# Attention scores of a diffusion layer: the low part of the queries multiplies only the high part of the keys, two key blocks in the two row halves of the array

## The chip, the cores and the metric

The kernel runs on one core of a Trainium2 chip. The metric is the device time of one execution, in microseconds (us); of several runs the median is given. A profile is one further execution with the hardware profiler on. Its own time stands beside its span, the time from its first to its last recorded instruction.

## The reference: what is computed

One layer of a diffusion backbone over 1024 latent tokens of width 1024, with 256 context tokens in front. Each layer normalizes and modulates the tokens, projects them with one combined matrix, feeds the columns to two groups of heads (chunkwise retention, and differential attention), projects their outputs back, and ends with a gated MLP with a short convolution. The change lies in the differential attention, cut here to what matters:

```python
def diff_attention(q, k, v, lam):
    """q (B,H,2,Lq,d), k (B,H,2,Lk,d), v (B,H,Lk,dv); softmax(q1k1)-lam*softmax(q2k2)."""
    scale = d ** -0.5
    def attend(qb):
        s = jnp.einsum('bhmqd,bhmkd->bhmqk', qb, k).astype(jnp.float32) * scale
        p = jax.nn.softmax(s, axis=-1)
        a = p[:, :, 0] - lam * p[:, :, 1]
        return jnp.einsum('bhqk,bhke->bhqe', a.astype(v.dtype), v)
...
    k_all = jnp.concatenate([dk_c, dk_l], axis=3)
    v_all = jnp.concatenate([dv_c, dv_l], axis=2)
```

There are H = 4 heads, two score maps m = 0, 1 per head, a head width d = 64, 1024 queries (latent tokens) and 1280 keys (256 context, 1024 latent). Softmax and the sum over keys do not depend on the order of the keys, as long as the keys and the values have the same order.

## The kernel before, in words

**Stages.** The kernel runs in this order: modulation vectors and normalized inputs; the input projection, weight block by weight block, with the retention worked beside it; the differential attention (from some 496 us to 695 us of the profile); the output projection; the two MLP products. Weight and token operands are split into a high part, rounded to the fast matmul type, and a low part, the rest; `passes` (L126 to L131) multiplies high by high, high by low and low by high.

**Queries and keys of the attention.** They are made by `transposed` (L433) and `rotated` (L407), which ends in `split_store` (L400). That one copies the high part into slot 0 of a tile `xhl` on ScalarE, the low part into slot 1 on VectorE, and writes both to DRAM through SyncE's queue. `dq_d[h]` and `dk_d[h]` in DRAM have the shape 64 x 2 (map m) x 2 (slot) x tokens. Of the keys, the context's come first (L625, columns 0 to 255) and the latents' behind them (L627, from column 256). The values `dv_d` have the same order (L568 and L605). Both halves `hf` of 512 latent tokens are handled alike.

**How they lie on the chip.** `load` (L796), through GpSimd's queue, fills the key tile `ks` as 128 partitions x 2 maps x 1280 keys: partitions 0 to 63 hold slot 0 (the high part of the 64 dimensions) and partitions 64 to 127 hold slot 1 (the low part). The query tile `qhl` holds the same queries in both partition halves: index i = 0 is the high part, i = 1 the low part. So one matmul over 128 partitions gives query part i times high plus low keys.

**One unit of the attention** is one head and one block of 128 queries, 32 units in all (`class Unit`, L714). `scores` (L722 to L727) fills, for one map m, the PSUM tile `pA` (1280 of 1536 columns, three banks) in three column blocks of 512, 512 and 256, each with two matmuls (i = 0 starts the sum, i = 1 ends it): six weight loads and six matmuls over the full array. Then follow `least` (the minimum over the keys, VectorE, L730), `exp` (ScalarE, L734), `ratio` and `combine` (the two maps into one, VectorE, L742), `turn` and `turned` (10 transposes on TensorE, L747, copied out by ScalarE, L753), `values` (the product with the values in full float32, 20 matmul instructions, L759), and the normalization of the output.

**What sets the order.** The units are pipelined: `TAU` (L64) gives every step a due time in units, and the loop at L865 issues, turn by turn, the steps of several units sorted by the fraction of their due time. `in_order` (L117) then fixes this order on TensorE, VectorE, ScalarE and SyncE. On TensorE one turn is: scores of map 1, four transposes, the 20 matmuls with the values, two transposes, scores of map 0, four transposes, the transpose of an output (`pty`, L782). There is one `pA` tile per map, so the scores of a map wait until `exp` of the unit before has read the tile. The early steps of the first two units (`EARLY`, L62) are issued at L821, between the last blocks of the query projection.

**A product elsewhere that splits the array.** The modulation vectors (`mod_part`, L488 to L499) are made with weights of 32 columns only. Four such matmuls write four groups of 32 PSUM partitions, so each uses a quarter of the array's columns. They stand between ordinary matmuls of the first projection.

Of the kernel before, what the change touches and what calls it, by code (L numbers as in the profile page):

```python
# [12 lines left out]
ALU = mybir.AluOpType  # L13
# [7 lines left out]
L = 1024  # L21
NT = L // P
LC = 256
NTC = LC // P
LK = LC + L
# [42 lines left out]
def r32(ap):  # L68
    return ap.bitcast(F32)
# [3 lines left out]
def kernel(  # L73
# [16 lines left out]
    nc = tc.nc  # L90
    mm = nc.tensor.matmul
# [34 lines left out]
    def passes(ps, lt, rt, first, last, more=False):  # L126
        lh, ll = lt
        rh, rl = rt
        mm(ps, lh, rh, start=first, stop=False, skip_group_check=more)  # L129
        mm(ps, lh, rl, start=False, stop=False, skip_group_check=more)  # L130
        mm(ps, ll, rh, start=False, stop=last, skip_group_check=more)  # L131
# [6 lines left out]
    dk_d = [dr.tile([64, 2, 2, LK], F32, name=f"dk{h}") for h in range(H)]  # L138
# [13 lines left out]
    with ExitStack() as p1:  # L152
        pctx = p1.enter_context(ExitStack())
        first = ExitStack()
# [10 lines left out]
        def mm_tile(name):  # L165
            return next(banks["mm"]).tile([P, 512], F32, name=name, tag="mm")
# [23 lines left out]
        def stream_parts(b):  # L190
            sl = []

            def more():
                kk = len(sl)
                sl.append(split_slice(w_in[b][:, 2 * kk : 2 * kk + 2, :]))

            def get(k, c0, c1):
                return tuple(t[:, k % 2, c0:c1] for t in sl[k // 2])

            return get, more  # L200

        def stream_block(b):
            get, more = stream_parts(b)
            for _ in range(KD // 2):
                more()
            return get
# [10 lines left out]
        def load_rope(kind):  # L217
            rtab = rp.tile([P, 2, L], F32, name="rtab")
            nc.sync.dma_start(out=rtab, in_=rope[:, kind])
            return rtab  # L220
# [147 lines left out]
        def tick():  # L368
            side["due"] += side["rate"]
            while side["due"] >= 1.0:  # L370
                side["due"] -= 1.0
                next(side["g"], None)

        def beside(g, rate, due=0.0):
            for _ in side["g"]:
                pass
            side.update(g=g, rate=rate, due=due)

        def natural(wget, lhs, tiles, finish):
            for t in tiles:  # L380
                pt = mm_tile("pn")
                for k in range(KD):
                    passes(pt, lhs(t, k), wget(k, 0, 512), k == 0, k == KD - 1)
                    tick()
                finish(t, pt)

        def store_to(dst, func=AF.Copy, scale=1.0, c0=0, center=False):
            def fin(t, pt):
                st = ev.tile([P, 4, P], F32, name="st", bufs=3)
                nc.scalar.activation(st.rearrange("p h e -> p (h e)"), pt, func, scale=scale)  # L390
                if center:
                    mu = ev.tile([P, 32], F32, name="mu")[:, 0:4]
                    nc.vector.tensor_reduce(out=mu, in_=st, axis=AX.X, op=ALU.add)
                    nc.vector.tensor_scalar(out=mu, in0=mu, scalar1=1.0 / P, scalar2=None, op0=ALU.mult)
                    nc.vector.tensor_tensor(out=st, in0=st, in1=mu.unsqueeze(2).to_broadcast([P, 4, P]), op=ALU.subtract)
                nc.sync.dma_start(out=dst(c0 + t), in_=st.rearrange("p h e -> p (h e)"))

            return fin

        def split_store(src, dst):  # L400
            n = src.shape[-1]
            hl = ev.tile([P, 2, 512], F32R, name="xhl")
            nc.scalar.copy(hl[:, 0, :n], src)
            nc.vector.tensor_tensor(out=hl[:, 1, :n], in0=src, in1=r32(hl[:, 0, :n]), op=ALU.subtract)
            nc.sync.dma_start(out=dst.rearrange("p m a l -> (p m) a l"), in_=r32(hl[:, :, :n]))

        def rotated(pt, dst, rtab, blk, scale, col0, h, hf):  # L407
            xa = ev.tile([P, 512], F32, name="xa")
            xb = ev.tile([P, 512], F32, name="xb")
            for q in (0, 64):  # L410
                nc.scalar.activation(xb[q : q + 64, :], pt[64 - q : P - q, :], AF.Copy, scale=scale)
            cs = rtab[:, 0, hf * 512 : (hf + 1) * 512]
            sn = rtab[:, 1, hf * 512 : (hf + 1) * 512]
            nc.vector.scalar_tensor_tensor(out=xa, in0=pt, scalar=scale, in1=cs, op0=ALU.mult, op1=ALU.mult)
            nc.vector.tensor_tensor(out=xb, in0=xb, in1=sn, op=ALU.mult)
            nc.vector.tensor_tensor(out=xa, in0=xa, in1=xb, op=ALU.add)
            c0 = col0 + hf * 512
            if blk == 32:
                split_store(xa, dst[h][:, :, :, c0 : c0 + 512])
            else:  # L420
                nc.sync.dma_start(out=dst[h][:, c0 : c0 + 512], in_=xa)
            return xa

        def natural_copy(xa, h, hf):
            pk = pst.tile([P, 4, P], F32, name="pk", tag="tr")
            for i in range(4):
                nc.tensor.transpose(pk[:, i, :], xa[:, i * P : (i + 1) * P], ident)
            st = ev.tile([P, 4, P], F32, name="st", bufs=3)
            nc.scalar.copy(st, pk)
            for i in range(2):  # L430
                nc.sync.dma_start(out=kvg_d[1 + 2 * hf + i][:, 0, :, h * P : (h + 1) * P], in_=st[:, 2 * i : 2 * i + 2, :])

        def transposed(wget, dst, rtab, blk, scale, col0, order, nat=False):  # L433
            todo = None
            for h, hf in order:
                pt = mm_tile("pl")
                for k in range(KD):
                    passes(pt, wget(k, h * P, (h + 1) * P), tuple(hT[a][hf][:, k, :] for a in range(2)), k == 0, k == KD - 1)
                    tick()
                    if todo and k == KD - 2:  # L440
                        natural_copy(*todo)
                xa = rotated(pt, dst, rtab, blk, scale, col0, h, hf)
                todo = (xa, h, hf) if nat else None
            if todo:
                natural_copy(*todo)
# [27 lines left out]
        by_head = [(h, hf) for h in range(H) for hf in range(2)]  # L473
        m2c = p1.enter_context(ExitStack())

        with ExitStack() as p0:
# [57 lines left out]
            wget, more = stream_parts(6)  # L534
# [30 lines left out]
                    modulate(xs, d, 0, hT[0][1][:, d, :], hT[1][1][:, d, :])  # L565
                    yield

            store = store_to(dv_row, c0=NTC)  # L568
            for i in range(2):
                for q in range(2):  # L570
                    t = 2 * i + q
# [30 lines left out]
                for t in ts:  # L602
                    store(t, part[t])
            side["rate"] = 0.6
            natural(wget, ctx_lhs, range(NTC), store_to(dv_row))  # L605
            beside(iter(()), 0.0)
        rc = late.enter_context(tc.tile_pool(name="rc", bufs=1))
        gn = rc.tile([P, 2, 512], F32, name="gn")
# [9 lines left out]
        rtab = load_rope(1)  # L618
        natural(wget, lat_lhs, range(4, NT), store)
        wg = stream_block(5)  # L620
        for h in range(H):
            pt = mm_tile("pc")
            for k in range(KD):
                passes(pt[:, :LC], wg(k, h * P, (h + 1) * P), tuple(cT[a][:, k, :] for a in range(2)), k == 0, k == KD - 1)
            split_store(pt[:, :LC], dk_d[h][:, :, :, 0:LC])  # L625
        modulation2(0)
        transposed(wg, dk_d, rtab, 32, 1.0, LC, by_head)  # L627
        with tc.tile_pool(name="rc0", bufs=1) as r0:
            lp = r0.tile([P, 4, 64], F32, name="lp")
            nc.sync.dma_start(out=lp.rearrange("p a b -> p (a b)"), in_=rows[0, R_LAM : R_LAM + 256].partition_broadcast(P))  # L630
# [44 lines left out]
        wg = stream_block(2)  # L675
# [3 lines left out]
        wg = stream_block(1)  # L679
# [5 lines left out]
        rtab = load_rope(0)  # L685
# [3 lines left out]
        wg = stream_block(3)  # L689
# [7 lines left out]
        wg = stream_block(0)  # L697
        beside(outputs(), 1.19, -14.5)
        transposed(wg, [q[:, 0] for q in rqk_d], rtab, 64, 1.0, 0, by_head)
        rtab = load_rope(1)  # L700
        wg = stream_block(4)
# [12 lines left out]
        class Unit:  # L714
# [7 lines left out]
            def scores(self, m):  # L722
                self.pa[m] = pss[m].tile([P, 1536], F32, name="pA")
                qs = slice(self.qt % 4 * P, (self.qt % 4 + 1) * P)
                for c0, c1 in ((0, 512), (512, 1024), (1024, LK)):
                    for i in range(2):
                        mm(self.pa[m][:, c0:c1], self.q[:, m, i, qs], self.k[:, m, c0:c1], start=(i == 0), stop=(i == 1))  # L727

            def least(self, m):
                nc.vector.tensor_reduce(out=self.mt[:, m : m + 1], in_=self.pa[m][:, :LK], axis=AX.X, op=ALU.min)  # L730
# [128 lines left out]
    with ExitStack() as p2:  # L859
# [3 lines left out]
        start = len(nc.cur_bb.bb.instructions)  # L863
        order = sorted(TAU.items(), key=lambda it: it[1] % 1.0)
        for n in range(n_units + 8):  # L865
# [6 lines left out]
            if n in (8, 10, 12, 14):  # L872
                a, i = divmod(n // 2 - 4, 2)
# [98 lines left out]
    with ExitStack() as p3:  # L972
        ps = p3.enter_context(tc.tile_pool(name="ps3", bufs=2, space=PSUM))
        for n in range(2):
# [3 lines left out]
            for t in range(NT):  # L978
                pt = ps.tile([P, 512], F32, name="po3", tag="mm")
# [3 lines left out]
                dst = x1[t][:, n * 512 : (n + 1) * 512]  # L983
# [75 lines left out]
    chain, second, first, fifth, third = {}, {}, {}, {}, {}  # L1059
# [25 lines left out]
    with ExitStack() as p4:  # L1085
# [79 lines left out]
        last = None  # L1165
        for j in range(NF):
# [8 lines left out]
            last = blk  # L1175
# [5 lines left out]
        def flat(t):  # L1181
            return t.rearrange("p a b -> p (a b)")
# [9 lines left out]
        c1 = [bank(f"c1_{t}", psB if t < 2 else psC) for t in range(4)]  # L1192
        c2 = [bank(f"c2_{t}", psA) for t in range(4)]
        for m in range(2):
            pa = flat(raw_load("wra", a_d[0][m].rearrange("p c (a b) -> p (c a) b", b=P)))
# [228 lines left out]
```

## Time and profile before

| | |
|---|---|
| median of 3 runs | 1433.39 us (1433.27 to 1436.08) |
| profiled execution | 1438.13 us, span 1436.3 us |
| mean granted TensorE clock | 0.989 |
| TensorE matmul busy | 1380.4 us, 96% of the span |
| TensorE weight loads busy | 1144.8 us, 80% |
| VectorE busy | 994.2 us, 69% |
| ScalarE busy | 728.8 us, 51% |
| GpSimd busy | 288.2 us, 20% |

How to read a profile: PE is TensorE's matmuls, PEld its weight loads, DVE VectorE, ACT ScalarE, POOL GpSimd, SP SyncE. L727 is line 727 of the kernel, and `out<-in` names the tiles that an instruction writes and reads. A timeline row gives the start, the time from the first start to the last end, the engine, the line and the count of merged instructions. The recorded time of a matmul is longer than the distance to the next one, since matmuls are pipelined; costs on TensorE are therefore read from start to start. The chain is the sequence of work that ended last, followed back from the end.

### The profile page before, as it was taken

The page shows a single profiled execution, that of the slowest core. Times are in us where ns is not written, and L with a number is a line of the kernel's source. Part 1 is how long each engine was busy: PE and PEld are TensorE (multiplying, and loading weights), DVE is VectorE, ACT ScalarE, POOL GpSimd, SP SyncE. Part 2 cuts the span into 40 slices and gives each one's busy share as a digit, 9 for nine tenths or more (in the row PEclk, how much of TensorE's full clock was granted, in tenths as well). Part 3 has the DMA queues.
Part 4 walks back from the last instruction along what each step waited for, and adds up shares of the span by engine and source line. Part 5 has one row for each costly group of instructions (what it writes and reads, how often), then busy time and mean ns, then how long its engine had stood idle before and what let it go on. Part 6 is the DMA issues. An engine that isn't in the chain of part 4 may idle for free.

```text
span 1436.3 us, 19187 instructions
## 1 busy us (share of the span) xinstructions
PE 1380.4 (96%) x6924; PEld 1144.8 (80%) x6924; DVE 994.2 (69%) x1432; ACT 728.8 (51%) x1386; POOL 288.2 (20%) x321
## 2 busy tenths in 40 slices
PE   6899999999989899999999999999999999999996
PEld 2687887788878789999888778888888888888885
DVE  3566755343666599888346997888778777998457
ACT  3534412343465488998314754555555545455533
POOL 1220000000645323431201143222222330000001
PEclk9999999999999999999999999999999999999998
DMA  8557755365465767570512222223222235953224
GB/s 313 220 178 243 250 180 190 115 194 176 136 208 192 202 149 174 132 146 1 220 52 88 74 95 108 98 110 110 102 86 88 108 110 174 397 204 102 98 96 175
DMA packets 109798, 218.79 MB, mean 152 GB/s; under 512 B 9156, under 2 KB 49604, under 8 KB 108808
## 3 DMA queue, kind: packets, MB, share of 16 engines
q1 hardware_dynamic: 101544, 192.67, 38.7%
q0 software_dynamic: 8160, 24.91, 7.7%
q8 instruction: 54, 0.88, 0.3%
q14 instruction: 40, 0.33, 0.1%
HBM read 160.13 MB, written 57.41 MB: 151 GB/s over the span
## 4 chain that ended last, share of the span: by engine, by line
PE 78%; DVE 7%; issue 5%; DMA 5%; ACT 2%; POOL 2%; SPq 0%; POOLq 0%; DVEq 0%; ACTq 0%
PE chain L129 5%; PE chain L130 5%; PE chain L131 5%; PE pv L759 5%; PE pA L727 4%; PE c L130 4%; PE c L131 4%; PE c L129 4%; PE pn L130 3%; PE pn L129 3%; PE pn L131 3%; PE pl L131 3%; PE pl L130 3%; PE pl L129 3%; PE third L130 2%
## 5 line engine op out<-in xcount | busy, mean ns | idle before, releaser
L129 PE MATMUL chain<-T,whi 128*128 128x512 f32 x264 | 103.7, 394 | 4.7 <-ACT ua L1140 3.9
L129 PE MATMUL pl<-hT,whi 128*128 128x512 f32 x256 | 108.2, 422 | 0.0
L130 PE MATMUL chain<-T,whi 128*128 128x512 f32 x264 | 103.5, 392 | 0.0
L131 PE MATMUL chain<-T,wlo 128*128 128x512 f32 x264 | 103.1, 391 | 0.0
L131 PE MATMUL pl<-hT,wlo 128*128 128x512 f32 x256 | 101.8, 398 | 0.0
L130 PE MATMUL pl<-hT,whi 128*128 128x512 f32 x256 | 101.7, 397 | 0.0
L730 DVE TENSOR_REDUCE mt<-pA 128x1 f32<-128x1280 f32 x64 | 95.1, 1489 | 3.0 <-PE pA L727 1.2
L727 PE MATMUL pA<-ks,qhl 128*128 128x512 f32 (+1 forms) x384 | 89.6, 369 | 2.2 <-ACT p L734 2.2
L131 PE MATMUL c<-whi,ghl 128*128 128x512 f32 x232 | 90.4, 390 | 0.0
L130 PE MATMUL c<-wlo,ghl 128*128 128x512 f32 x232 | 90.3, 389 | 0.0
L129 PE MATMUL c<-whi,ghl 128*128 128x512 f32 x232 | 90.3, 389 | 0.0
L734 ACT ACTIVATE p<-pA,mt 128x1280 f32<-128x1280 f32 x64 | 85.5, 1336 | 8.4 <-DVE mt L730 8.3
L898 ACT CAST whi<-cmb 128x512 fp32r<-128x512 f32 x62 | 38.6, 622 | 86.5 <-PE chain L130 66.9
L129 PE MATMUL pn<-whi,hT 128*128 128x512 f32 x192 | 79.2, 412 | 0.0
L727 PEld LDWEIGHTS pA<-ks,qhl 128*128 128x128 f32 x384 | 67.6, 189 | 14.4 <-ACT p L734 3.0
L1053 POOL TENSOR_TENSOR cmb<-wrb 128x512 f32<-128x512 f32 x20 | 27.8, 1392 | 247.7 <-DMA wrb<-w_up 155.6
L759 PE MATMUL pv<-va,aT 128*128 128x128 f32 x640 | 77.1, 276 | 0.1
L130 PE MATMUL pn<-wlo,hT 128*128 128x512 f32 x192 | 76.2, 397 | 0.0
L131 PE MATMUL pn<-whi,hT 128*128 128x512 f32 x192 | 75.3, 395 | 0.5 <-DVE hT L531 0.5
L899 DVE TENSOR_TENSOR wlo<-cmb,whi 128x512 fp32r<-128x512 f32 x62 | 59.5, 963 | 23.2 <-ACT whi L898 23.2
L759 PEld LDWEIGHTS pv<-va,aT 128*128 128x128 f32 x640 | 74.0, 192 | 1.0 <-DVE yT L788 0.6
L115 POOL TENSOR_TENSOR sm<-sm,mhalf 128x1 f32<-128x1 f32 x26 | 16.1, 619 | 278.3 <-DVE sm L114 278.1
(302 smaller groups left out, 3820.5 us busy)
## 6 DMA issues: line engine op xcount, KB each, us to landing
wm<-w_mod SPq DMA_DIRECT2D x32, 512.0 KB, 4.4
raw<-w_in SPq DMA_DIRECT2D x28, 512.0 KB, 4.3
wra<-w_up SPq DMA_DIRECT2D x24, 512.0 KB, 3.3
wrb<-w_up SPq DMA_DIRECT2D x23, 512.0 KB, 3.6
W<-w_down SPq DMA_DIRECT2D x44, 256.0 KB, 5.9
ad<-s SPq DMA_DIRECT2D x20, 512.0 KB, 3.5
wra<-ad SPq DMA_DIRECT2D x20, 512.0 KB, 3.4
kvs<-kvg SPq DMA_DIRECT2D x36, 256.0 KB, 3.3
```

What stands on the lines that cost most here:

```text
L115: nc.gpsimd.tensor_tensor(out=out_ap, in0=out_ap, in1=mhalf[:, :n], op=ALU.pow)
L129: mm(ps, lh, rh, start=first, stop=False, skip_group_check=more)
L130: mm(ps, lh, rl, start=False, stop=False, skip_group_check=more)
L131: mm(ps, ll, rh, start=False, stop=last, skip_group_check=more)
L727: mm(self.pa[m][:, c0:c1], self.q[:, m, i, qs], self.k[:, m, c0:c1], start=(i == 0), stop=(i == 1))
L730: nc.vector.tensor_reduce(out=self.mt[:, m : m + 1], in_=self.pa[m][:, :LK], axis=AX.X, op=ALU.min)
L734: nc.scalar.activation(self.p[m], self.pa[m][:, :LK], AF.Exp, scale=-1.0, bias=self.mt[:, m : m + 1], accum_out=self.s[:, m : m + 1])
L759: mm(self.pv, self.aT[:, c, :], self.v[:, c, :], start=(c == 0), stop=(c == NKT - 1))
L898: nc.scalar.copy(hi, src)
L899: nc.vector.tensor_tensor(out=lo, in0=src, in1=r32(hi), op=ALU.subtract)
L1053: nc.gpsimd.tensor_tensor(out=s1, in0=b1, in1=b2, op=ALU.add)
```

## The change

The low part of the queries no longer multiplies the low part of the keys in the first two key blocks. For these 1024 keys the i = 0 matmul stays as it was, over all 128 partitions. The i = 1 matmuls become two matmuls over 64 partitions each: key block 0 takes partitions 0 to 63 of query and key, key block 1 takes partitions 64 to 127. So that the high part of the keys lies in the right half, the latent keys move to the front (columns 0 to 1023, the context behind them), and the second half of the latents stores its low part in slot 0 and its high part in slot 1. The last block of 256 keys, now the context, keeps both full matmuls, and they are issued ahead of the two half ones. The values in DRAM follow the new order of the keys.

```diff
-        def split_store(src, dst):
+        def split_store(src, dst, first=0):
             n = src.shape[-1]
             hl = ev.tile([P, 2, 512], F32R, name="xhl")
-            nc.scalar.copy(hl[:, 0, :n], src)
-            nc.vector.tensor_tensor(out=hl[:, 1, :n], in0=src, in1=r32(hl[:, 0, :n]), op=ALU.subtract)
+            nc.scalar.copy(hl[:, first, :n], src)
+            nc.vector.tensor_tensor(out=hl[:, 1 - first, :n], in0=src, in1=r32(hl[:, first, :n]), op=ALU.subtract)
             nc.sync.dma_start(out=dst.rearrange("p m a l -> (p m) a l"), in_=r32(hl[:, :, :n]))
...
-                split_store(xa, dst[h][:, :, :, c0 : c0 + 512])
+                split_store(xa, dst[h][:, :, :, c0 : c0 + 512], hf if dst is dk_d else 0)
...
-            store = store_to(dv_row, c0=NTC)
+            store = store_to(dv_row)
...
-            natural(wget, ctx_lhs, range(NTC), store_to(dv_row))
+            natural(wget, ctx_lhs, range(NTC), store_to(dv_row, c0=NT))
...
-            split_store(pt[:, :LC], dk_d[h][:, :, :, 0:LC])
+            split_store(pt[:, :LC], dk_d[h][:, :, :, L:LK])
         modulation2(0)
-        transposed(wg, dk_d, rtab, 32, 1.0, LC, by_head)
+        transposed(wg, dk_d, rtab, 32, 1.0, 0, by_head)
...
             def scores(self, m):
                 self.pa[m] = pss[m].tile([P, 1536], F32, name="pA")
                 qs = slice(self.qt % 4 * P, (self.qt % 4 + 1) * P)
-                for c0, c1 in ((0, 512), (512, 1024), (1024, LK)):
-                    for i in range(2):
-                        mm(self.pa[m][:, c0:c1], self.q[:, m, i, qs], self.k[:, m, c0:c1], start=(i == 0), stop=(i == 1))
+                pa = self.pa[m]
+                for c0, c1, last in ((0, 512, False), (512, 1024, False), (1024, LK, True)):
+                    for i in range(1 + last):
+                        mm(pa[:, c0:c1], self.q[:, m, i, qs], self.k[:, m, c0:c1], start=(i == 0), stop=(i == 1))
+                for g in range(2):
+                    half = slice(64 * g, 64 * g + 64)
+                    mm(pa[:, 512 * g : 512 * g + 512], self.q[half, m, 1, qs], self.k[half, m, 512 * g : 512 * g + 512], start=False, stop=True)
```

## The prediction

> **What bounds the kernel now.** The page's first part says that TensorE is busy for 96% of the span, but that is a mean. I therefore went to the table by stages for the attention, where the only edited instructions that cost time lie. Its columns after the stretch are its length, then the busy time (and count) of PE, PEld, DVE, ACT and POOL, the granted clock, the DMA share and GB/s.
>
> ```profile
> PE 1380.4 (96%) x6924; PEld 1144.8 (80%) x6924; DVE 994.2 (69%) x1432; ACT 728.8 (51%) x1386; POOL 288.2 (20%) x321
> ...
> 550.00:590.00 40.00, 40.00 (x299) 37.37 (x298) 35.78 (x50) 36.08 (x87) 12.44 (x25) 1.00 0.64 160
> 590.00:630.00 40.00, 39.89 (x294) 36.37 (x292) 34.54 (x49) 38.01 (x89) 18.59 (x29) 1.00 0.75 142
> 630.00:670.00 40.00, 40.00 (x299) 37.55 (x300) 36.14 (x49) 35.81 (x84) 6.17 (x17) 1.00 0.20 41
> ```
>
> TensorE has no free time in these stretches. ScalarE and VectorE are close behind, with 36 of 40 us, and 38 where ScalarE also casts output weights. Busy PE need not be the bound, so next I read the chain of work that ended last, once for 510 to 700 us (first row) and once for 640 to 690 us (the rest): start, duration, engine, tile, line, count.
>
> ```profile
> by line: PE pv L759 35.6%; PE pA L727 33.1%; PE pt L747 16.8%; DVE mt L730 3.0%; PE pty L782 2.2%; ACT p L734 2.1%; PE po L129 0.9%; PE po L130 0.9%; PE po L131 0.8%; DVE p L742 0.8%; issue 0.8%; ACT aT L753 0.7%; ACT jka L768 0.4%; ACT oa
> ...
> 643.37 2.23 PE pv L759 x20
> 645.60 0.22 PE pt L747 x2
> 645.82 1.16 PE pA L727 x6
> 646.98 0.44 PE pt L747 x4
> 647.52 1.16 PE pA L727 x6
> 648.68 0.44 PE pt L747 x4
> 649.12 2.23 PE pv L759 x20
> ```
>
> One turn takes 649.12 - 643.37 = 5.75 us and is TensorE from end to end: 2.23 + 0.22 + 1.16 + 0.44 + 1.16 + 0.44, and 0.10 between 647.42 and 647.52. So a microsecond more or less in L727 is a microsecond of the kernel, in nearly every turn. How many of the 64 score steps lie on this chain: 33.1% of 190 us is 62.9 us, and at 1.16 us each that is **54**. The other ten lie at the two ends, where the scores wait for ScalarE, as these two of the early steps do:
>
> ```profile
> 504.88 1.22 PEld L727 LDWEIGHTS pA<-ks,qhl 128*128 128x128 f32 x6 [1.16 <-ACT p L734]
> 506.95 1.22 PEld L727 LDWEIGHTS pA<-ks,qhl 128*128 128x128 f32 x6 [0.84 <-ACT p L734]
> ```
>
> **The change part by part.** *Stores and order of the keys.* The copies, subtractions and DMAs of `split_store`, the value stores and the loads keep their number, size, engine and queue; only addresses and the slot differ. I put this at nothing. No queue is passed, and no wait is added.
>
> *Scores.* There are six weight loads and six matmuls before and after. Before, the columns fed are 4 x 512 + 2 x 256. After, the full array is fed 2 x 512 + 2 x 256, and two matmuls of 512 columns use 64 rows each. The price of a full matmul is read from start to start in the first projection, and that of a block of 256 from the end of one score step:
>
> ```profile
> 44.13 0.39 PE L130 MATMUL pn<-wlo,hT 128*128 128x512 f32 x1
> 44.36 0.39 PE L131 MATMUL pn<-whi,hT 128*128 128x512 f32 x1
> 44.68 1.07 PE L499 MATMUL pr<-wt,cz 128*32 128x512 f32 x8
> 45.67 0.50 PE L129 MATMUL pn<-whi,hT 128*128 128x512 f32 x1
> 46.01 0.39 PE L130 MATMUL pn<-wlo,hT 128*128 128x512 f32 x1
> 46.24 0.39 PE L131 MATMUL pn<-whi,hT 128*128 128x512 f32 x1
> ```
> ```profile
> 593.34 0.40 PE L727 MATMUL pA<-ks,qhl 128*128 128x256 f32 x2
> 593.57 0.27 PE L747 MATMUL pt<-ident,p 128*128 128x128 f32 x1
> ```
>
> A full matmul of 512 columns costs 44.36 - 44.13 = 0.23 us, its weight load hidden under the one before, and two of 256 cost 593.57 - 593.34 = 0.23 us. Four of 512 and two of 256 make 5 x 0.23 = 1.15 us, which agrees with the 1.16 of the chain.
>
> **The gain:** if both halves run at the same time, one of the two costs nothing. That takes 0.23 us away per score step.
>
> **The cost:** no instruction in this profile splits the rows of the array. The nearest rows are those just shown: L499 splits its columns into four tiles, between ordinary matmuls, so they price both the running at the same time and the change over. Whether the tiles run together is seen from two narrow windows of the same place:
>
> ```profile
> 44.68 0.64 PE L499 MATMUL pr<-wt,cz 128*32 128x512 f32 x4
> ...
> 45.13 0.61 PE L499 MATMUL pr<-wt,cz 128*32 128x512 f32 x4
> ```
>
> The eight instructions are two waves of four. All of the first four start between 44.68 and the window's edge at 44.70, and the next four 0.45 us later, at 45.13. So tiles do run together, with at most 0.02 us between first and last. I take 0.23 + 0.02 = 0.25 us for the pair of halves.
>
> The way in: after 44.36 the next ordinary matmul would have started at 44.59; L499 starts at 44.68, **0.09 us** late. The way out: the second wave is fed until 45.13 + 0.45 = 45.58; the next matmul starts at 45.67, another **0.09 us**. And that matmul is 0.34 us ahead of its successor in place of 0.23 (46.01 - 45.67), because its weights were not loaded ahead:
>
> ```profile
> 44.14 0.19 PEld L131 LDWEIGHTS pn<-whi,hT 128*128 128x128 f32 x1
> 44.68 0.16 PEld L499 LDWEIGHTS pr<-wt,cz 128*32 128x32 f32 x8 [0.35 <-issue]
> 45.67 0.19 PEld L129 LDWEIGHTS pn<-whi,hT 128*128 128x128 f32 x1 [0.84 <-issue]
> 45.78 0.19 PEld L130 LDWEIGHTS pn<-wlo,hT 128*128 128x128 f32 x1
> ```
>
> L129's load starts only with its own matmul at 45.67, while L130's is already there 0.11 us later, under L129. So **0.11 us** of load stands bare after a change of mode. On the way in L499 shows nearly none of it, as its weights have 32 columns; the half matmuls' weights have 128, like L129's, so I charge 0.11 us on the way in too. The price is not an accident of one place:
>
> ```profile
> 39.26 0.40 PE L131 MATMUL pn<-whi,hT 128*128 128x512 f32 x1
> 39.58 1.05 PE L499 MATMUL pr<-wt,cz 128*32 128x512 f32 x4
> 40.56 0.50 PE L129 MATMUL pn<-whi,hT 128*128 128x512 f32 x1
> 41.00 1.05 PE L499 MATMUL pr<-wt,cz 128*32 128x512 f32 x4
> 41.98 0.51 PE L130 MATMUL pn<-wlo,hT 128*128 128x512 f32 x1
> 42.32 0.39 PE L131 MATMUL pn<-whi,hT 128*128 128x512 f32 x1
> ```
>
> Here too the way in is 39.58 - 39.26 - 0.23 = 0.09, and the matmul behind the way out takes 42.32 - 41.98 = 0.34. The type (L499 is plain float32) isn't the reason: scores of the fast type are followed by float32 transposes at 593.57 without any such gap.
>
> The Trainium skill has the same thing as a rule: in "TensorEngine Tiling (Array Packing)", section Key Properties, a change of the tiling mode, unlike a change of the tile, drains TensorE. It gives no price; the 0.09 us of the trace agrees with it, for columns.
>
> **The sum** per score step on the chain: 0.09 + 0.11 in, 0.25 for the pair, 0.09 + 0.11 out, less the 2 x 0.23 of the two matmuls that go: 0.65 - 0.46 = **+0.19 us**. Every score step is followed by four transposes, so the way out is paid each time. Over 54 steps that is +10.3 us. For the other ten I take nothing: there TensorE waits anyway, the way out falls into the wait, and up to the last score 0.20 + 0.25 - 0.46 is about zero.
>
> Could a stall absorb part of it? The two largest waits of its matmuls from 496 to 696 us are these (who waits, for whom, total us, times, longest):
>
> ```profile
> PE pA L727 <- ACT p L734: 2.2, 3, 0.8
> PE pt L747 <- ACT aT L753: 1.1, 2, 0.6
> ```
>
> The first lies in the early steps; at most 1.1 us of the second could vanish. I leave it in the error. VectorE and ScalarE, at 36 of 40 us now, only get more room from a longer turn.
>
> The profiled execution would go from 1438.13 to 1448.4 us. It was 4.7 us above the median of the runs shown, so on that median: 1433.39 + 10.3 = **1443.7 us**.
>
> **Both ends of the unknown.** Row tiles are not column tiles. Below: the change of mode costs nothing for rows, -0.23 + 0.02 = -0.21 us. Above: the two halves do not overlap at all, 0.40 us of changes over and no gain. I take the column rows' value, since they are the only rows of this kernel in which the array changes its division.
>
> **The rivals.**
>
> *Faster: no change-over for row halves.* Each half's weights are loaded under the full matmul before, and nothing is drained. Then a step saves 0.21 us, 54 steps 11.3 us. A turn would be 5.75 - 0.42 = 5.33 us. ScalarE needs 36.08 / 40 x 5.75 = 5.19 us per turn, but 38.01 / 40 x 5.75 = 5.46 us where it casts; in some nine such turns 0.13 us each, 1.2 us, is lost again. That gives about 1423.3 us. It decides as soon as the changes over cost less than 0.21 us together. For it speaks that in ordinary matmuls loads always go ahead; against it, each change over in the rows above. The Trainium skill speaks for it in part: "TensorEngine Tiling (Array Packing)", section Theoretical Speedup, gives up to 2x where a dimension is at most 64. Chance 0.18.
>
> *The same: drained, but loaded ahead.* Only 2 x 0.09 remains: 0.18 - 0.21 = -0.03 us a step, -1.6 us, 1431.8 us. About 0.2%, or 2.9 us, is what a measurement of this kernel can tell from no change. Against it stands the start of L129's load at 45.67. Chance 0.12.
>
> *Slower still: the change doesn't do what it says.* If the loads of the halves follow one another, the second half starts 0.11 us later in place of 0.02: +0.28 us a step, +15 us, 1448.5 us. If the halves run one behind the other, two matmuls of 0.23 stay and only the changes over are added: +0.40 us a step, +21.6 us, 1455.0 us. For it: two halves read two different weight sets and write two PSUM banks, and no row here shows that. Against it: the four tiles that start together at 44.68. Chance 0.20, both.
>
> **How the numbers follow.** The forecast, a price per step between 0.14 and 0.25 us or 1441 to 1447 us, has 0.50. Slower by over 0.2% then has 0.50 + 0.20 = 0.70, within 0.2% 0.12, faster 0.18. The range leaves out the faster rival (0.18) and reaches from below the same case to above the slowest: 1429 to 1458 us. Cases of both signs do not share the chance evenly, and the forecast's own range lies wholly on the slow side.
>
> **What would show it.** In the profile after, the turn from one group of 20 L759 matmuls to the next should be 5.75 + 0.38 = 6.13 us. The first half should start some 0.20 us behind the last full matmul of 256 columns, in place of 0.11, and its weight load with it, not under the full matmul. The second half should start within 0.02 us of the first. The first transpose behind them should stand 0.11 us further from its successor than before. DVE and ACT should fall from 36 to about 34 of 40 us in the same stretches. The forecast is wrong if the half loads are seen under the full matmuls, or if the starts of the halves are 0.23 us apart.

## The result and the profile after

The change makes the kernel **slower by 0.26%**: the median is 1439.82 us (1435.32 to 1445.03, 22 runs) against 1435.63 us (1431.16 to 1440.45, 22 runs) of the kernel before on the same chips; the ratio is 1.0026 with a 95% interval of 1.0017 to 1.0036. On 1435.6 us that is +3.7 us, between +2.4 and +5.2 (the two medians lie 4.2 us apart, within that interval). The forecast was +10.3 us: the sign was right, the size was not.

Single executions of one kernel spread over 9 to 10 us, more than the effect. The profiled execution of after even has a shorter span, 1434.8 us against 1436.3, because its attention began 6.7 us earlier (489.52 against 496.19 us), before any edited matmul. That need not come from the edited stores: among the runs below whose code up to there is that of after, the first score matmul stands anywhere from 486.4 us (one full matmul in place of the pair) to 499.5 us (the change of mode alone). So only the attention itself is compared here. First the table by stages of after, with the columns as above:

```profile
550.00:590.00 40.00, 40.00 (x292) 33.98 (x291) 34.93 (x48) 34.75 (x83) 13.35 (x25) 1.00 0.68 157
...
630.00:670.00 40.00, 40.00 (x286) 33.57 (x286) 35.48 (x47) 33.69 (x82) 6.19 (x16) 1.00 0.16 27
```

TensorE is still full. VectorE and ScalarE have fallen, from 36 to about 35 and 34 of 40 us, since fewer units fit into 40 us. Next the chain of after, 640 to 690 us; L763 are the matmuls with the values, L728 the full score matmuls, L731 the halves, L751 the transposes.

```profile
640.50 2.23 PE pv L763 x20
642.95 0.70 PE pA L728 x4
643.65 0.43 PE pA L731 x2
644.07 0.58 PE pt L751 x4
...
646.48 2.23 PE pv L763 x20
```

One turn takes 646.48 - 640.50 = 5.98 us in place of 5.75, and is still all TensorE. Half of the difference of 0.23 is one score step: it costs **0.115 us** more, not 0.19. A piece of the chain runs from the end of the piece before to its own end. So 0.70 is the feeding of the four full matmuls, 0.43 the way in and the feeding of the pair, and 0.58 the way out and the transposes, which were 0.44 before.

The place itself, in a narrow window of the timeline of after (the last full matmul, the loads and the matmuls of the halves), and then, from a wider one, what follows:

```profile
594.85 0.28 PE L728 MATMUL pA<-ks,qhl 128*128 128x256 f32 x1
595.05 0.19 PEld L731 LDWEIGHTS pA<-ks,qhl 64*128 64x128 f32 x2
595.06 0.50 PE L731 MATMUL pA<-ks,qhl 64*128 64x512 f32 x2
```
```profile
595.49 0.66 PE L751 MATMUL pt<-ident,p 128*128 128x128 f32 x4
595.98 0.27 PE L786 MATMUL pty<-ident,oa 128*128 128x128 f32 x1
```

The window shown ends at 595.08, so both halves and both of their loads start by then. They come 0.21 us behind the last full matmul in place of 0.11, so 0.10 us passes in draining, and their weights are loaded only then, 0.11 us bare. From the halves to the first transpose it is 0.43 us: 0.11 of load, 0.23 of feeding, 0.09 of draining. From there to `pty` it is 0.49 us. In the kernel before it was 0.44:

```profile
593.57 0.60 PE L747 MATMUL pt<-ident,p 128*128 128x128 f32 x4
...
594.01 0.27 PE L782 MATMUL pty<-ident,oa 128*128 128x128 f32 x1
```

So the transposes' bare load is 0.05 us, where I had charged 0.11.

### The profile page after: what moved, and what is told of

Same layout as the page of the kernel before. It is cut to its first block, busy times and chain, and to the rows that moved or that the text cites. A ratio compares the mean times of both kernels' runs of the same rounds, so it can differ in the third digit from the quotient of the medians.

```text
span 1434.8 us, 19187 instructions
## 1 busy us (share of the span) xinstructions
PE 1384.6 (97%) x6924; PEld 1132.5 (79%) x6924; DVE 993.3 (69%) x1432; ACT 727.6 (51%) x1386; POOL 288.4 (20%) x321
## 4 chain that ended last, share of the span: by engine, by line
PE 78%; DVE 6%; DMA 5%; issue 5%; POOL 2%; ACT 2%; SPq 0%; POOLq 0%; DVEq 0%; ACTq 0%
PE pv L763 5%; PE chain L129 5%; PE chain L131 5%; PE chain L130 5%; PE c L131 4%; PE c L129 4%; PE c L130 4%; PE pt L751 3%; PE pA L728 3%; PE pl L131 3%; PE pn L130 3%; PE pl L129 3%; PE pl L130 3%; PE pn L129 3%; PE pn L131 3%
## 5 line engine op out<-in xcount | busy, mean ns | idle before, releaser
L129 PE MATMUL chain<-T,whi 128*128 128x512 f32 x264 | 103.7, 394 | 4.7 <-ACT ua L1144 3.9
L129 PE MATMUL pl<-hT,whi 128*128 128x512 f32 x256 | 107.2, 419 | 0.0
L129 PE MATMUL c<-whi,ghl 128*128 128x512 f32 x232 | 90.4, 389 | 0.0
L129 PE MATMUL pn<-whi,hT 128*128 128x512 f32 x192 | 79.4, 414 | 0.0
L763 PE MATMUL pv<-va,aT 128*128 128x128 f32 x640 | 77.0, 276 | 0.0
L763 PEld LDWEIGHTS pv<-va,aT 128*128 128x128 f32 x640 | 74.0, 192 | 0.7 <-DVE yT L792 0.4
L902 ACT CAST whi<-wra 128x512 fp32r<-128x512 f32 x55 | 33.7, 622 | 71.7 <-PE third L130 42.3
L129 PE MATMUL third<-yT,whi 128*128 128x512 f32 x168 | 65.4, 389 | 0.0
```

What stands on the lines that cost most here:

```text
L763: mm(self.pv, self.aT[:, c, :], self.v[:, c, :], start=(c == 0), stop=(c == NKT - 1))
L902: nc.scalar.copy(hi, src)
```

## The experiments

**My theory after the result (A):** the two halves overlap fully; each change of mode drains TensorE for 0.10 us and leaves the next weight load bare, which is 0.11 us for score weights and 0.05 us for a transpose. Per step 0.10 + 0.43 + 0.05 = 0.58 us in place of 2 x 0.23. **Rivals:** the halves overlap only in part while their load is hidden (B); the other engines hold the turn, so that even a free change over would bring nothing (C); the way out costs the same whatever follows (D); the cost sits in the half matmuls, not in the change of mode (E, F); part of the loss comes from the stores.

"Turn" is the distance between the starts of two neighbouring groups of 20 matmuls with the values, the median over the attention, read from the trace.

### One half only

```diff
...
-                for g in range(2):
+                for g in range(1):
```

> The second half matmul is left out, so the low queries never meet key block 1. Theory A (the two halves overlap fully; each score step pays about 0.10 us of draining and 0.11 us of bare weight load on the way in, 0.10 us of draining and a bare load of what follows on the way out): the turn stays at 5.985 us (within 0.03), the time at +4 us against before. Rival B (the load on the way in is hidden, and what is seen as load is the second half starting 0.11 us behind the first): the turn falls by 2 x 0.11 to 5.77 us, the time to about that of before.

The turn is 5.97 us, the ratio to before 1.0036 (1.0018 to 1.0055), no different from that of after. The chain:

```profile
647.04 0.69 PE pA L728 x4
647.73 0.43 PE pA L731
```

The way in and one half take 0.43 us, as with two. The second half is free; B falls. The Trainium skill, "TensorE: Matmul & The Clock Gate", section "Measured speedup vs the span model", gives about 4 ns for each further tile. Here the turn of after is 0.02 us longer than this one, for two second halves, so about 10 ns each: also small, but more than the Trainium skill's figure.

### Both halves in the same rows

```diff
-                    half = slice(64 * g, 64 * g + 64)
+                    half = slice(0, 64)
```

> Both half matmuls use rows 0 to 63, so key block 1 meets the wrong part of the keys. Theory A: the halves can no longer overlap, each step grows by one feeding of 512 columns, 0.22 us; turn 6.43 us, time +4 + 29 x 0.45 = about +17 us against before. Rival B (partial overlap now): 0.11 us a step, turn 6.2 us, about +10 us.

The turn is 6.44 us, the ratio 1.0121 (1.0088 to 1.0153), +17 us, as A has it.

```profile
648.41 0.69 PE pA L728 x4
649.10 0.66 PE pA L731 x2
```

In the same rows the way in and the pair take 0.66 us in place of 0.43: the second is fed behind the first, 0.23 us. The overlap is thus a matter of different rows, and the second load hides in both cases.

### A full matmul in place of the pair

```diff
...
-                for g in range(2):
-                    half = slice(64 * g, 64 * g + 64)
-                    mm(pa[:, 512 * g : 512 * g + 512], self.q[half, m, 1, qs], ...)
+                mm(pa[:, 0:512], self.q[:, m, 1, qs], self.k[:, m, 0:512], start=False, stop=True)
```

> One full matmul over 128 rows (low queries, key block 0) in place of the two halves; the low queries never meet key block 1. No change of mode, as many full feedings as a free change over would leave. Theory A: TensorE's work per turn falls by 2 x 0.23 to 5.30 us; ScalarE needs 5.19 to 5.46 us, so the turn comes to 5.35 to 5.45 us and the time to about -9 us against before (-0.6%). Rival C (the other engines already hold the turn at 5.7 us): at most -2 us.

The ratio is 0.9968 (0.9951 to 0.9984), -4.6 us: faster, but half of what A gave. The turn is 5.51 us, where A had 5.30 us of work for TensorE and a turn of 5.35 to 5.45. The chain, and what holds it (the waits of TensorE's weight loads, 550 to 670 us):

```profile
645.50 0.23 PE pA L729
645.74 0.44 PE pt L749 x4
646.18 2.45 PE pv L761 x20
```
```profile
PEld pv L761 <- DVE yT L790: 4.1, 19, 0.5
```

The score steps are 0.23 us shorter, but 0.2 us a turn comes back in front of the matmuls with the values: 2.45 in place of 2.23, since they wait for VectorE's last step of an older output (`yT`), which frees their PSUM buffer (`pt`, `pv` and `pty` share two in the kernel). C holds by half: by these waits it is not the busy time of another engine, but a wait in the fixed order, that takes part of the gain. By this run a change over at no cost would have been worth some 5 us here (2.3 to 7.0), not 10; my faster rival was priced too high, as it looked at busy times only.

### The pair ahead of the last key block

```diff
-                for c0, c1, last in ((0, 512, False), (512, 1024, False), (1024, LK, True)):
+                for c0, c1, last in ((0, 512, False), (512, 1024, False)):
...
                 for g in range(2):
...
+                for i in range(2):
+                    mm(pa[:, 1024:LK], self.q[:, m, i, qs], self.k[:, m, 1024:LK], start=(i == 0), stop=(i == 1))
```

> The pair of halves stands ahead of the two matmuls of 256 columns, not behind them, so that a score matmul (weights load 189 ns) and not a transpose (141 ns) follows the way out. Same work. Theory A: the bare load on the way out grows from 0.055 to 0.11 us, +0.055 us a step, turn 6.095 us, time about +7 us against before. Rival D (the way out costs the same whatever follows): turn 5.985 us, +4 us.

The turn is 6.10 us (A: 6.095), the ratio 1.0060 (1.0036 to 1.0084), +8.6 us.

```profile
647.83 0.47 PE pA L728 x2
648.29 0.43 PE pA L731 x2
648.73 0.43 PE pA L733 x2
649.16 0.44 PE pt L753 x4
```

The transposes are back at 0.44, so the way out now lies in front of the two full matmuls of L733. These take 0.43 in place of 0.23. Of the 0.20, 0.11 is bare load, since the second of the two starts 0.22 us behind the first (648.66 and 648.88) where 256 columns take 0.11; the other 0.09 is draining. The transposes of after paid 0.58 - 0.44 = 0.14. By the turn, the same work costs 0.06 us a step more because of what follows the way out. D falls; this is the term that the prediction had too large.

### The new layout alone

```diff
-                for c0, c1, last in ...
-                for g in range(2):
...
+                for c0, c1 in ((0, 512), (512, 1024), (1024, LK)):
+                    for i in range(2):
+                        mm(self.pa[m][:, c0:c1], self.q[:, m, i, qs], self.k[:, m, c0:c1], start=(i == 0), stop=(i == 1))
```

> The new order of keys and values and the new slots, with the six full matmuls of before: the change without its half matmuls. If stores and order of the keys cost nothing (the prediction's step): turn 5.755 us, time within 0.1% of before. Rival: part of the +4 us comes from the stores, then this run shows it, at least +1.5 us.

The turn is 5.75 us, the ratio 0.9992 (0.9978 to 1.0007). The new order of keys and values and the swapped slots cost nothing that can be measured.

### The change of mode alone

Against the kernel with the new layout alone:

```diff
                 for c0, c1 in ((0, 512), (512, 1024), (1024, LK)):
-                    for i in range(2):
+                    for i in range(1 + (c0 > 0)):
                         mm(pa[:, c0:c1], self.q[:, m, i, qs], ...)
+                mm(pa[:, 0:512], self.q[0:64, m, 1, qs], self.k[0:64, m, 0:512], start=False, stop=True)
```

> The new layout with full matmuls, except that the low queries of key block 0 use one half matmul (rows 0 to 63), issued last. So as many columns are fed one after the other as before, and only the change of mode is added; the low by low product of block 0 is left out. Theory A, with the prices read from the change: 0.10 draining and 0.11 bare load in, 0.09 draining and 0.05 bare load out, +0.35 us a step; turn 5.755 + 0.70 = 6.45 us, time about +18 us against before (28 turns x 0.70, less 1.5 of stalls). Rival F (the 0.10 and 0.09 are a property of two tiles at once, not of the change of mode): only the loads remain, +0.16 us a step, turn 6.08 us, +7 us.

The turn is 6.45 us, as A said; the ratio is 1.0138 (1.0109 to 1.0168), +20 us.

```profile
608.50 2.23 PE pv L761 x20
...
610.95 0.93 PE pA L728 x5
611.89 0.42 PE pA L729
612.31 0.59 PE pt L749 x4
...
614.95 2.23 PE pv L761 x20
```

As many columns are fed as before, and only one of the six matmuls has 64 rows. That alone costs (6.45 - 5.755) / 2 = **0.35 us a step**, the price of going in and out. Rival F falls. So does E: with one half in place of two the step costs the same, as the run with one half showed. Against it stand the 0.23 us that the overlap of the pair saves: 0.35 - 0.23 = 0.12, the step of after.

### Two changes over per step

```diff
...
+                for g in range(2):
+                    half = slice(64 * g, 64 * g + 64)
+                    mm(pa[:, 512 * g : 512 * g + 512], self.q[:, m, 0, qs], self.k[:, m, 512 * g : 512 * g + 512], start=True, stop=False)
+                    mm(pa[:, 512 * g : 512 * g + 512], self.q[half, m, 1, qs], self.k[half, m, 512 * g : 512 * g + 512], start=False, stop=True)
+                for i in range(2):
+                    mm(pa[:, 1024:LK], self.q[:, m, i, qs], self.k[:, m, 1024:LK], start=(i == 0), stop=(i == 1))
```

> The same products as the change, but each half matmul behind the full matmul of its own block, so that a full matmul stands between the halves: two changes over per step and no overlap. Theory A: each lone half costs 0.10 + 0.11 + 0.23 + 0.09 and the score matmul behind it 0.11 of bare load, 0.64 us in place of 0.23 or 0.0: two cost 1.28 us against the pair's 0.58, +0.70 us a step; turn 5.985 + 1.40 = 7.38 us, time about +44 us against before. Rival G (with halves in different rows a lone half still overlaps the full matmul beside it): at most half of that, turn 6.7 us.

The turn is 7.35 us (A: 7.38), the ratio 1.0353 (1.0317 to 1.0388), +51 us where A had +44. The turns bring what A gave. The rest lies in the early steps, which A left out: from the first score matmul to the first with the values it is 24.4 us, before 17.8; why stays open. One step in the timeline:

```profile
603.58 0.50 PE L729 MATMUL pA<-ks,qhl 64*128 64x512 f32 x1
604.01 0.50 PE L728 MATMUL pA<-ks,qhl 128*128 128x512 f32 x1
604.43 0.50 PE L729 MATMUL pA<-ks,qhl 64*128 64x512 f32 x1
604.86 0.51 PE L731 MATMUL pA<-ks,qhl 128*128 128x256 f32 x2
```

Between a half and a full matmul every matmul of 512 columns takes 0.43 us from start to start in place of 0.23, in either direction. So the price belongs to each change, and it adds up. G falls: a lone half does not run beside a full matmul. The same 0.43 us lies between the halves and the transposes of after, so no wait for another engine hides in that one.

### One change over for two steps

Since a change costs 0.35 us and a pair saves 0.23, two pairs per change should pay. For this the scores of both maps have to stand together. The first kernel is the one before with only the scores moved, the second is the change with the halves behind the scores of both maps, the third also pairs the context's 256 keys of the two maps (for which it loads those of map 1 with high and low part swapped).

```diff
-TAU = dict(S0=0.6383, ...
+TAU = dict(S0=0.9990, ...
```

> The kernel before with one due time changed: the scores of map 0 are issued directly ahead of the scores of map 1 of the next unit. No half matmuls. It is the control for the next two. TensorE's work is the same; turn 5.755 us and time within 0.2% of before, unless the new order makes TensorE wait for a minimum or an exponential, which would show as idle time of PE.

```diff
-EARLY = ("S1", "M1", "S0", "M0", "E1", "E0", "R", "C")
+EARLY = ("S1", "H1", "M1", "S0", "H0", "M0", "E1", "E0", "R", "C")
-TAU = dict(S0=0.6383, ...
+TAU = dict(S0=0.9990, H0=1.0010, H1=0.0020, ...
+            def halves(self, m):
...
```

> The change with the scores of both maps next to each other and their four half matmuls behind one another, so that one change over serves two steps. Theory A: one way in and one way out less per turn, 0.10 + 0.11 + 0.10 + 0.055 = 0.36 us: turn 5.985 - 0.36 = 5.62 us, 0.13 us under before, about -4 us (-0.3%). Rival E (the cost sits in each half matmul, not in the change of mode): turn 5.985 us, +4 us.

```diff
-TAU = dict(S0=0.9990, H0=1.0010, H1=0.0020, ...
+TAU = dict(S0=0.9990, H0=1.0010, H1=0.0020, X0=1.0030, X1=0.0031, ...
+            def context(self, m):
+                half = slice(64 * m, 64 * m + 64)
+                mm(self.pa[m][:, 1024:LK], self.q[half, m, 1, qs], self.k[half, m, 1024:LK], start=False, stop=True)
...
```

> The same, and the context's 256 keys too meet the low queries only with their high part: map 0 in rows 0 to 63, map 1 in rows 64 to 127, as a third pair. Two full matmuls of 256 columns (0.115 us each) become one pair (0.115 us). Theory A: another 0.115 us a turn, turn 5.51 us, about -7 us against before (-0.5%). Rival: ScalarE, at 5.46 us in turns with a cast, stops the turn at 5.6 us and the time at about -4 us.

All three are much slower, the control too: ratios 1.0263 (1.0245 to 1.0281), 1.0391 (1.0373 to 1.0410) and 1.0455 (1.0433 to 1.0478), turns 7.17, 7.84 and 7.95 us. My expectation of the control failed, so these times say nothing on the change over. The chain of the control shows why:

```profile
566.67 1.50 DVE mt L730
...
568.20 1.42 ACT p L734 x2
569.62 0.48 ACT aT L753
570.09 1.32 ACT p L734 x2
571.41 0.17 ACT oa L763
...
571.62 0.66 PE pt L747 x4
...
572.31 0.33 PE pty L782
572.64 1.17 PE pA L727 x6
...
573.84 1.50 DVE mt L730
```

The scores now stand behind the transposes and `pty` in TensorE's order. The transposes wait for ScalarE's copy `oa`, which frees a PSUM buffer that they need; in ScalarE's order this copy comes behind the exponentials of both maps; and these wait for the minima, which wait for the scores. All of it hangs on this one ring of 7.17 us. In the second kernel the ring is longer still, since there the minimum waits for the full matmuls of both maps and its own two halves:

```profile
567.51 1.39 PE pA L728 x8
568.90 0.44 PE pA L735 x2
```

That is 1.83 us in place of 1.17, which is the 0.67 us between the turns of the two. TensorE's own part did get shorter, as A has it; in the timeline of the second kernel:

```profile
567.26 1.64 PE L728 MATMUL pA<-ks,qhl 128*128 128x512 f32 x8
568.83 0.73 PE L735 MATMUL pA<-ks,qhl 64*128 64x512 f32 x4
569.49 0.66 PE L755 MATMUL pt<-ident,p 128*128 128x128 f32 x4
```

Four halves take 569.49 - 568.83 = 0.66 us, 0.23 more than two. Whether another order can keep this without the ring stays open; it wasn't tried. No version here that keeps the products of the change is faster than the kernel before.

## Why the prediction was right and wrong

**Right.** TensorE bounds the attention, and each step is paid in the turn. The halves overlap, the tiles' rows of L499 carried over from columns to rows: drained for 0.10 and 0.09 us, load bare on the way in for 0.11 us, both starts within 0.02 us. The stores and the order of the keys cost nothing. The ten steps at the ends cost nearly nothing: from the first score matmul (496.19 before, 489.52 after) to the second group with the values on the chain it is 24.45 us before and 24.60 us after (520.64 and 514.12, the rows of the chain below).

```profile
496.19 1.30 PE L727 MATMUL pA<-ks,qhl 128*128 128x512 f32 x6
```
```profile
489.52 0.85 PE L728 MATMUL pA<-ks,qhl 128*128 128x512 f32 x4
```

**Wrong: the size of one term,** "0.09 + 0.11 out". I had read the bare load of 0.11 us behind L129, a projection matmul, and charged it to "four transposes", though I had named them as what follows. A transpose's weights load in 141 ns where a score matmul's take 188, and both rows were in the profile before:

```profile
L727 PEld LDWEIGHTS pA<-ks,qhl x384: 186/188/248, 496.0 to 681.1; 128*128 128x128 f32 x192
```
```profile
L747 PEld LDWEIGHTS pt<-ident,p x320: 138/141/148, 508.8 to 691.3; 128*128 128x128 f32 x160
```

The bare load is 0.05 us, and the run with the pair ahead of the last key block shows the difference, 0.06 us a step. The allowance of 0.02 us for the second half was also too much, as the run with one half shows. Together: 0.19 - 0.06 - 0.02 = 0.11 to 0.12 us a step, below the forecast's own band of 0.14 to 0.25. Over 54 steps that takes 4 of the 10.3 us away, 3 of them by the bare load.

**Wrong by a little: the stall left in the error.** From the second group with the values to the one at 683 us the chain of before, and that of after, run thus:

```profile
520.64 2.23 PE pv L759 x20
...
683.34 2.50 PE pv L759 x20
```
```profile
514.12 2.23 PE pv L763 x20
...
681.89 2.50 PE pv L763 x20
```

That is 162.70 us before and 167.77 after, +5.1 us for 28 turns, of which 27 have their full 0.23 us more, 6.2 us. So 1.1 us came back: in the kernel before TensorE waits in some turns, mostly where ScalarE also casts (turns of 5.94, 6.05, 6.18 and 6.27 us among those of 5.75), and the longer turn takes up part of that. I had named 1.1 us as the most that could vanish and had not subtracted it. That the size agrees is luck, since it was another wait. The one that I had named, of the transposes for `aT`, is still there after the change. Some 0.7 us of what went is the wait of the weight load of `pty`; the prediction had listed the waits of the matmuls alone (from 496 to 696 us; the first two rows are of after, the last of before):

```profile
PE pt L751 <- ACT aT L757: 1.0, 2, 0.6
PEld pty L786 <- ACT aT L757: 0.3, 1, 0.3
PEld pty L782 <- ACT aT L753: 1.0, 5, 0.3
```

54 steps at 0.115 us less 1.1 us give 5.1 us, at the upper end of the measured +2.4 to +5.2; whether anything else came back stays open.

**The rivals.** The faster one falls with the first rows of after: no half load starts while the full matmul before is fed (595.05 against 594.85 + 0.11). Its price was too high as well (4.6 us measured for a free change over, 10 us said). The same case fails on the bare load, the slower ones on the overlap. The rule of "TensorEngine Tiling (Array Packing)", section Key Properties, in the Trainium skill, that a change of mode drains TensorE, holds for row tiles too: 0.10 us.

## What to carry to other kernels

Split rows or columns of the array only where what runs together per change saves more than the change costs: here 0.35 us in and out, against 0.23 us for one pair of 512 columns, so one pair loses; two pairs would save 0.46. When a cost is carried over from another place, take also what stands behind it there and here: the same drained pipeline exposed 0.11 us in front of one kind of weights and 0.05 us in front of another. And before steps are moved together to share a cost, follow the ring of buffer, producer and consumer through the fixed order: it took 7.17 us where the engine needed 5.75.

## What the runs showed of the hardware

- A change between full and half rows costs the same in both directions apart from the load behind it: 0.43 us from start to start for a matmul of 512 columns in place of 0.23, three times in a step of the run with two changes.
- Two matmuls of 64 rows in the same rows run one behind the other with the second load hidden (0.66 us with two, 0.43 with one), so it is the change of mode, and not the half height, that bares a load.
